# Expert stage of a mixture-of-experts block on one core: TensorE's order written by hand, and the second expert weight read in 8 KB runs

## The chip, the cores and the metric

One NeuronCore of one Trainium2 chip runs the whole block in one launch. The metric is the device time in microseconds (us). Lower is better. Three runs of the kernel before took 1494.55, 1496.63 and 1498.79 us; the median is 1496.63 us.

## The reference, cut to what matters

One layer of a diffusion backbone: modulated norm, a combined projection, two token mixers, an output projection, and then the part that the change touches, a mixture of 32 experts over 256 tokens of 1024 channels. Every token goes to its 4 best experts.

```python
def expert_block(args):                       # for every expert e, on its tokens
    xblk, e = args
    z = xblk @ w1[e] + b1[e]                  # w1: (32, 1024, 2048), float32
    gate = jnp.minimum(z[:, :D_EXPERT], SWIGLU_LIMIT)
    lin = jnp.clip(z[:, D_EXPERT:], -SWIGLU_LIMIT, SWIGLU_LIMIT)
    return (gate * jax.nn.sigmoid(SWIGLU_ALPHA * gate) * (lin + 1.0)) @ w2[e] + b2[e]   # w2: (32, 1024, 1024)
...
x = x + g2 * moe_ffn(modulate(x, norm2_g, sh2, sc2), ...)     # weighted sum of each token's experts
return rms_norm(x, final_g)
```

All weights are float32 and are read once: 8 MiB of w1 and 4 MiB of w2 for each expert, 384 MiB for the 32.

## The kernel before, in words

The first third (to about 500 us) computes the modulation, the projections, the mixers and the router, and isn't touched. The rest is the expert stage.

**Tiles.** Every expert has 64 slots (C = 64; a branch behind the loop serves experts with more tokens). `expert_rows` selects the tokens of two experts at a time and `gather` (L769) brings their activations into `xT2`, [channel, slot]. `expert_in` computes the first product: `zz` are two PSUM banks, gate and lin, opened by four small bias products (L791); then each of 8 tiles of w1 (128 rows of 2048 floats, 1 MiB, DMA at L795) is used by 4 products (L798), which stand in the trace as 8 MATMULs. The swiglu follows on VectorE and ScalarE (L803 to L807), the result is turned by four transposes (L810) and copied out by ScalarE (L812) as `hT2`. `expert_out` opens the bank `py` (L820), uses 4 tiles of w2 (1 MiB each, DMA at L824) with 8 MATMULs each (L828), multiplies by the gate g2 (`y`, L831), and scatters `y` back to the tokens with a one-hot matrix `pT` from `spread` (L780): four products (L840), each added into `acc` on VectorE (L843). The last expert's second product goes by columns, 256 at a time (`expert_out_by_columns`, L851 to L866), so that the final norm can begin early.

**The ring.** All weight tiles go through one ring of buffers of 8 KB a partition, in program order (`wtile`). SyncE (SP) issues their DMAs; each waits until TensorE has read the tile that had the buffer before. For the last two experts two buffers leave the ring, to hold rows that the end needs.

**The order.** Nothing in the expert stage is ordered by hand: the program is recorded expert by expert, and a scheduler with a simulated timeline places the instructions of each engine. In program order the second product of an expert stands right behind its swiglu.

**The layout of w2.** Row r of w2 sits on partition r % 128, so a tile of 256 rows gives each partition two runs of 4 KB:

```python
w = wtile([P, 2, D])
nc.sync.dma_start(w, w2e(k2).rearrange("(k p) n -> p k n", p=P))     # L824
```

A tile of w1 gives each partition one run of 8 KB; the last expert's column tiles give runs of 1 KB.

Of the kernel before, what the change touches and what calls it, by code (L numbers as in the profile page):

```python
# [16 lines left out]
P = 128  # L17
# [14 lines left out]
def kernel(  # L32
# [41 lines left out]
    def rstd_of(dst, ss, scale, tmp):  # L74
        """dst = (ss * scale + EPS) ** -0.5: a first guess from the exponent, then Newton steps."""
# [106 lines left out]
    def mod_sums(j, h):  # L182
        """Columns 512 h.. of part j for c, in two steps; still to be summed over partitions."""
# [65 lines left out]
    def modulation(q, w0=None):  # L249
        """md[:, j, a] = columns 256 q.. of part j (shift, scale) for c (a = 0) and c_ctx; a1 = (1 + scale) norm1_g"""  # L250
# [35 lines left out]
    class Granule:  # L286
        """256 columns of a (1024, n) matrix; pieces of k are split into two exact float32r parts."""
# [97 lines left out]
    def pair_dense(j, iv, q, og, sg):  # L385
        """The dense products of two heads, a granule a step."""
# [19 lines left out]
    def decays(hd, k, q):  # L406
        """The decayed queries and keys of a head; in [channel, token]."""
# [41 lines left out]
    def attend(hd, dec, iv, og):  # L449
        """Scores and states, output, and its norm and gate: three steps."""  # L450
# [299 lines left out]
    for tags, bufs in ((("sc0", "sc1", "py"), 1), (("gate",), 2), (("misc",), 1), (("lin",), 2)):  # L750
# [26 lines left out]
    def spread(sel, slot0):  # L777
        """[64 h + s, t] = 1 where token t has slot s + slot0 with the selected expert"""
# [6 lines left out]
    def expert_in(xT, selb, w1e):  # L785
        """swiglu(x w1 + b1) of the 64 tokens of xT; [channel, kt % 4, 64 (kt // 4) + slot]"""
# [6 lines left out]
        for kt in range(KT):  # L793
            w = wtile([P, 2 * D])
            nc.sync.dma_start(w, w1e(kt))  # L795
            for n in range(2):
                for h in range(2):
                    te.matmul(zz[n][h * C:(h + 1) * C], xT[:, kt], w[:, n * D + h * 512:n * D + (h + 1) * 512],  # L798
                              start=False, stop=kt == KT - 1, skip_group_check=True)
# [7 lines left out]
        ve.scalar_tensor_tensor(l, l, 1.0, g, op0=OP.add, op1=OP.mult)  # L807
        ph = bank2("misc", (P, 4, P))
        for k in range(4):
            te.transpose(ph[:, k], l[:, k * P:(k + 1) * P], ident)  # L810
# [4 lines left out]
    def expert_out(hT2, pT, selb, wcol, w2e, old=None):  # L815
        """acc = old + wcol * pT^T (g2 * (h w2 + b2))"""
# [14 lines left out]
        ve.tensor_mul(y, py, g2h)  # L831
        nonlocal acc
# [4 lines left out]
        for tt in range(2):  # L837
# [7 lines left out]
    def expert_out_by_columns(hT2, pT, selb, wcol, w2e):  # L845
        """The same, 256 columns at a time, with what the final norm needs of them; halves of py hold partial sums."""
        selb = selb.to_broadcast([96, C])
        for j in range(4):
            s = slice(j * 256, (j + 1) * 256)
            w = wtile([P, KT, 256])  # L850
            nc.sync.dma_start(w, w2e[:, s].rearrange("(k p) n -> p k n", p=P))  # L851
            py = bank2(("py", "misc")[j % 2], (P, 256))
            te.matmul(py[0:C], selb, b3[:, 2, s], start=True, stop=False, skip_group_check=True)
            for kt in range(KT):
                h = kt % 2
                te.matmul(py[h * C:(h + 1) * C], hT2[:, kt % 4, (kt // 4) * C:(kt // 4) * C + C], w[:, kt],
                          start=kt == 1, stop=kt >= KT - 2, skip_group_check=True)
            y = wk.tile([P, 256], F32, name="y")
            ve.tensor_mul(y, py, g2bc[:, s])
            for tt in range(2):  # L860
# [5 lines left out]
                (gp if j < 3 else ve).tensor_mul(accg[:, tt, s], acc[:, tt, s], fgbc[:, s])  # L866

    xT2 = p2 = None

    def expert_rows(e, n):  # L870
        """Selects and gathers for n experts from e."""
        m = e % 2
        for k in range(n):
            for tt in range(2):
                select(p2[:, tt, m + k], posm[:, tt, e + k:e + k + 1], tt)
        gather(p2[:, :, m:m + n].rearrange("p t a b -> p t (a b)"), xT2[:, :, m * C:(m + n) * C], n * C)

    late = []
    for e in range(E):
        if e == E - 2:  # L880
            slots[:] = [x for x in slots if x[1] not in ("d0", "d1")]
            bc = consts.tile([P, 2, D], F32, name="bc", tag="d0")
            fgbc, g2bc = bc[:, 0], bc[:, 1]
            gp.dma_start(fgbc, bcast(final_g, D))  # L884
            for h in range(2):
                pb = bank2("misc")
                te.matmul(pb, ident[:, h * C:h * C + 1].to_broadcast([P, P]), g2h, start=True, stop=True)
                sc.activation(g2bc[:, h * 512:(h + 1) * 512], pb, AF.Copy)
            accg = consts.tile([P, 2, D], F32, name="accg", tag="d1")
            ss8 = consts.tile([P, 2, 4], F32, name="ss8")  # L890
        if e % 2 == 0:
            p2 = wk.tile([P, 2, 2, C], F32, name="p2")
            xT2 = wk.tile([P, KT, 2 * C], F32, name="xT2")
            expert_rows(e, 1 if e == 0 else 2)
        elif e == 1:
            expert_rows(e, 1)
        if e == 0:
            ve.tensor_sub(lg, lg, view(top, 0, [[8, 2], [0, E]]))
            sc.activation(lg, lg, AF.Exp)
            ve.tensor_mul(wts, lg, mk)  # L900
            ve.reduce_sum(den, wts, axis=mybir.AxisListType.X)
            ve.reciprocal(den, den)
            for tt in range(2):
                ve.tensor_scalar(wts[:, tt], wts[:, tt], den[:, tt:tt + 1], None, op0=OP.mult)
        es = e % 2
        selb = sel96[:, e:e + 1]
# [3 lines left out]
        if e == E - 2:  # L910
            continue
# [96 lines left out]
```

## Time and profile before

| what | value |
|---|---|
| median of 3 runs | 1496.63 us (1494.55 to 1498.79) |
| span of the profiled execution | 1494.2 us |
| the profiled execution's own time | not listed apart; the three runs lie 0.4 to 4.6 us above its span, their median 2.4 us |
| PE busy over the span | 1371.3 us (92%) |
| DVE, ACT busy | 640.2 us (43%), 308.1 us (21%) |
| moved by DMA | 487.44 MB, mean 326 GB/s; 416 GB/s from 600 to 1395 us |

PE is TensorE's matmul, PEld its weight load, DVE VectorE, ACT ScalarE, SP SyncE. A MATMUL's end is modelled and neighbours overlap, so how long a kind of work takes is read from start to start in the timeline, not from the busy time. The DMA share is the busy share of the 16 DMA engines by the packets' own times; with two packets of an engine overlapping it goes over 1.

### The profile page before, as it was taken

How to read it: one execution, taken by the hardware profiler on the slowest of the kernel's cores; microseconds unless marked ns; L12 is line 12 of the kernel's file. 1: busy time of each engine (PE TensorE's matmuls, PEld its weight loads, DVE VectorE, ACT ScalarE, POOL GpSimd, SP SyncE). 2: the span in 40 equal slices, each digit the busy share in tenths (PEclk: the TensorE clock that was granted, in tenths of full speed). 3: DMA queues.
4: the chain of work that ended last, by engine and by line, in shares of the span. 5: the costliest groups of instructions: out<-in, count | busy, mean ns of one | idle time of the engine just before them, and what ended most of it. 6: DMA issues, size and time to landing. Idle time of an engine off the chain costs nothing. (4 is left out here: it accounts for less than half of the span.)

```text
span 1494.2 us, 19672 instructions
## 1 busy us (share of the span) xinstructions
PE 1371.3 (92%) x8218; PEld 760.8 (51%) x8218; DVE 640.2 (43%) x1108; ACT 308.1 (21%) x497; POOL 162.2 (11%) x109
## 2 busy tenths in 40 slices
PE   6979797979999989999999999998999989998996
PEld 4979797979999633343333233333333333333233
DVE  5598879697787421322323222222222222222124
ACT  3463535373444200000000000000000000001001
POOL 3054414240171000000000000000000000000001
PEclk8999999999999999999999999999999999999998
DMA  9536243435977799999999999999999999999970
GB/s 334 186 101 220 101 158 113 152 131 171 345 249 300 308 377 377 416 414 419 416 416 418 416 416 418 418 416 416 418 418 416 415 417 411 414 410 413 388 276 30
DMA packets 146560, 487.44 MB, mean 326 GB/s; under 512 B 9097, under 2 KB 71682, under 8 KB 113698
## 3 DMA queue, kind: packets, MB, share of 16 engines
q1 hardware_dynamic: 145618, 483.37, 83.1%
q0 software_dynamic: 848, 2.75, 0.6%
q8 instruction: 67, 1.10, 0.3%
q14 instruction: 27, 0.22, 0.0%
HBM read 485.04 MB, written 1.05 MB: 325 GB/s over the span
## 5 line engine op out<-in xcount | busy, mean ns | idle before, releaser
L798 PE MATMUL gate<-w,xT 128*64 128x512 f32 x1024 | 271.0, 598 | 4.0 <-DVE xT L775 4.0
L798 PE MATMUL lin<-w,xT 128*64 128x512 f32 x1024 | 272.1, 592 | 0.0
L828 PE MATMUL py<-w,hT 128*64 128x512 f32 x992 | 243.4, 634 | 16.1 <-ACT hT L812 16.1
L321 PE MATMUL acc<-hh,ghi 128*128 128x256 f32 x576 | 166.9, 290 | 12.1 <-ACT iv L394 12.1
L321 PE MATMUL acc<-hh,glo 128*128 128x256 f32 x576 | 165.5, 288 | 11.3 <-DVE glo L242 11.3
L321 PE MATMUL acc<-hl,ghi 128*128 128x256 f32 x576 | 165.1, 287 | 0.0
L242 DVE TENSOR_TENSOR glo<-w,ghi 128x1024 fp32r<-128x1024 f32 (+1 forms) x99 | 140.0, 1419 | 50.7 <-ACT ghi L241 50.3
L798 PEld LDWEIGHTS lin<-w,xT 128*64 128x64 f32 x1024 | 75.4, 137 | 148.4 <-issue 148.2
L828 PEld LDWEIGHTS py<-w,hT 128*64 128x64 f32 x992 | 71.2, 143 | 143.8 <-issue 115.9
L843 DVE SCALAR_TENSOR_TENSOR acc<-sc,wts,acc 128x512 f32<-128x512 f32 x124 | 89.0, 747 | 123.5 <-PE sc L840 123.4
L798 PEld LDWEIGHTS gate<-w,xT 128*64 128x64 f32 x1024 | 69.4, 136 | 127.1 <-issue 106.6
L241 ACT ACTIVATE ghi<-w 128x1024 fp32r<-128x1024 f32 (+1 forms) x102 | 102.3, 1007 | 144.6 <-PE acc L321 107.7
L321 PEld LDWEIGHTS acc<-hh,ghi 128*128 128x128 f32 x576 | 111.4, 194 | 13.3 <-ACT iv L394 12.5
L321 PEld LDWEIGHTS acc<-hh,glo 128*128 128x128 f32 x576 | 111.3, 193 | 12.9 <-DVE glo L242 12.6
L803 DVE TENSOR_SCALAR g<-gate 128x512 f32<-128x512 f32 x32 | 22.1, 692 | 212.1 <-PE gate L798 202.3
L321 PEld LDWEIGHTS acc<-hl,ghi 128*128 128x128 f32 x576 | 111.4, 193 | 0.7 <-issue 0.7
L804 ACT ACTIVATE s<-g 128x512 f32<-128x512 f32 x32 | 20.2, 630 | 423.6 <-DVE g L803 423.6
L884 POOL DMA_DIRECT2D bc<-in_final_g_dram x1 | 0.6, 557 | 934.7 <-DMA w<-in_w_dram 934.7
L831 DVE TENSOR_TENSOR y<-py,g2h 128x512 f32<-128x512 f32 x31 | 21.4, 692 | 165.0 <-PE py L828 165.0
L840 PE MATMUL sc<-y,pT 64*128 64x512 f32 x248 | 84.7, 641 | 8.0 <-DVE y L831 7.8
L321 PE MATMUL acc<-ghi,hh 128*128 128x256 f32 x256 | 73.3, 288 | 13.8 <-DVE og L383 6.3
L321 PE MATMUL acc<-glo,hh 128*128 128x256 f32 x256 | 73.1, 286 | 1.4 <-DVE glo L242 1.4
(320 smaller groups left out, 1656.1 us busy)
## 6 DMA issues: line engine op xcount, KB each, us to landing
w<-in_w_dram SPq DMA_DIRECT2D x384, 1024.0 KB, 13.7
w<-in_w_in_dram SPq DMA_DIRECT2D x33, 1024.0 KB, 5.7
w<-in_w_mod_dram SPq DMA_DIRECT2D x24, 1024.0 KB, 6.9
w<-in_w_branch_a_dram SPq DMA_DIRECT2D x4, 1024.0 KB, 16.3
w<-in_w_branch_b_dram SPq DMA_DIRECT2D x4, 1024.0 KB, 12.2
w<-in_w_out_dram SPq DMA_DIRECT2D x4, 1024.0 KB
w<-in_w_in_dram SPq DMA_DIRECT2D x12, 256.0 KB, 7.7
bt<-in_b_dram POOLq DMA_DIRECT2D x9, 128.0 KB, 5.0
```

What stands on the lines that cost most here:

```text
L241: sc.activation(hi, src, AF.Copy)
L242: eng.tensor_sub(lo, src, hi)
L321: te.matmul(o, l, r, start=opens and kt == 0 and n == 0, stop=kt == KT - 1 and n == 2, skip_group_check=True)
L798: te.matmul(zz[n][h * C:(h + 1) * C], xT[:, kt], w[:, n * D + h * 512:n * D + (h + 1) * 512], start=False, stop=kt == KT - 1, skip_group_c ...
L803: ve.tensor_scalar(g, zz[0], 7.0, None, op0=OP.min)
L804: sc.activation(s, g, AF.Sigmoid, scale=1.702)
L828: te.matmul(py[h * C:(h + 1) * C], hT2[:, kt % 4, (kt // 4) * C:(kt // 4) * C + C], w[:, k, h * 512:(h + 1) * 512], start=False, stop=kt = ...
L831: ve.tensor_mul(y, py, g2h)
L840: te.matmul(pcs[h], pT[h * C:(h + 1) * C, tt * P:(tt + 1) * P], y[h * C:(h + 1) * C], start=True, stop=True)
L843: ve.scalar_tensor_tensor(acc[:, tt, s], pcs[h], wcol[tt], old[:, tt, s], op0=OP.mult, op1=OP.add)
L884: gp.dma_start(fgbc, bcast(final_g, D))
```

## The change

`expert_in` and `expert_out` are cut into pieces (`w1_open`, `w1_step`, `swiglu`, `turned`, `w2_steps`, `scatter`, `last_columns`), and TensorE's instructions in the expert stage stand in the order in which the program writes them (`tc.manual_schedule`). The program now runs one expert behind with the second product: the first product of expert e, then its swiglu is recorded, then the second product of expert e - 1, then the transposes of e. The scatter of e - 2 stands behind the second and third tile of e's first product, and the gathers for the next two experts behind the fourth and sixth. The weights are allocated and read in that same order.

w2 is laid out anew: row 512 h + 4 p + k sits on partition p, so a tile gives each partition one run of 8 KB, and neighbouring partitions' runs lie 16 KB apart (the other half is read by the next tile). To match, the transposes read every fourth column of the swiglu's result. The last expert's column tiles keep runs of 1 KB, in two DMAs each. The PSUM pools change: gate and lin have one bank each in place of two, misc has three in place of one, and both halves of a gather go into misc. The two buffers leave the ring one expert later.

```diff
-    for tags, bufs in ((("sc0", "sc1", "py"), 1), (("gate",), 2), (("misc",), 1), (("lin",), 2)):
+    for tags, bufs in ((("sc0", "sc1", "py"), 1), (("gate",), 1), (("misc",), 3), (("lin",), 1)):
...
-    def gather(tok, xT, n):
-        for k4 in range(2):
-            pg = bank2(("misc", "sc0")[k4], (P, 4, n))
+    def gather(tok, xT, n, k4s=(0, 1)):
+        for k4 in k4s:
+            pg = bank2("misc", (P, 4, n))
...
+    def turned(l):
         ph = bank2("misc", (P, 4, P))
         for k in range(4):
-            te.transpose(ph[:, k], l[:, k * P:(k + 1) * P], ident)
+            te.transpose(ph[:, k], view(l, k, [[4, P]]), ident)
...
             w = wtile([P, 2, D])
-            nc.sync.dma_start(w, w2e(k2).rearrange("(k p) n -> p k n", p=P))
+            nc.sync.dma_start(w, w2e[:, k2 // 2, k2 % 2 * 2:k2 % 2 * 2 + 2])
...
-            nc.sync.dma_start(w, w2e[:, s].rearrange("(k p) n -> p k n", p=P))
+        for h in range(2):
+            nc.sync.dma_start(w[:, 4 * h:4 * h + 4], w2e[:, h, :, s])
...
+    w2e = lambda e: w2[0, e].rearrange("(h p k) n -> p h k n", h=2, k=4)
...
+    with tc.manual_schedule(engines={mybir.EngineType.PE}):
+        first_zz = w1_open(sel(0))
+        for f in rows_of(0, 1):
+            f()
+        for e in range(E):
...
+            zz = w1_open(sel(e)) if e else first_zz
+            for kt in range(KT):
+                w1_step(zz, xTs[e], kt, w1e(e, kt))
+                if kt in (1, 2) and ready:
+                    scatter(*ready[1:], x1 if ready[0] == 0 else None, (kt - 1,))
+                if kt == 3:
+                    steps = rows_of(1, 1) if e == 0 else rows_of(e + 1, 2) if e % 2 and e < E - 1 else []
+                if kt in (3, 5) and steps:
+                    steps[kt // 2 - 1]()
...
+            l = swiglu(zz)
+            if out_of:
+                pe, phT = out_of
+                pT = spread(identb[:, pe:pe + 1], 0)
+                y = w2_steps(phT, sel(pe), w2e(pe))
+                ready = pe, y, pT, wcols(pe)
+            out_of = e, turned(l)
+        e, hT2 = out_of
+        pT = spread(identb[:, e:e + 1], 0)
+        rest = last_columns(0, hT2, pT, sel(e), wcols(e), w2e(e))
+        scatter(*ready[1:])
+        for j in range(1, 4):
+            then = last_columns(j, hT2, pT, sel(e), wcols(e), w2e(e))
+            rest()
+            rest = then
+        rest()
```

TensorE at the turn from one expert to the next, in the middle of the stage, before. L791 opens the banks of the next first product, L810 are the transposes, L828 the second product, L780 the spread, L840 the scatter, L798 the next first product.

```order
L798 MATMUL lin<-w,xT_7833 64x512 x2
L791 LDWEIGHTS sel_69
...
L791 MATMUL lin<-b_4507,sel_69 64x512
L810 MATMUL misc<-ident,l 128x128 x4
L828 MATMUL py<-w,hT_7935 64x512 x8
L780 LDWEIGHTS identb
L780 MATMUL misc<-posT,identb 128x256
L828 MATMUL py<-w,hT_7935 64x512 x8
L840 MATMUL sc_7966<-y,pT 128x512
L840 MATMUL sc_7967<-y,pT 128x512
```

The same turn now (L800 is the first product, L836 the second, L818 the transposes, L852 the scatter).

```order
L800 MATMUL lin<-w,xT_7966 64x512 x2
L780 LDWEIGHTS identb
L780 MATMUL misc<-posT,identb 128x256
...
L836 MATMUL py<-w,hT_8067 64x512 x16
L818 MATMUL misc<-ident,l 128x128 x4
L791 LDWEIGHTS sel_69
...
L800 MATMUL gate<-w,xT_7966 64x512 x2
L800 MATMUL lin<-w,xT_7966 64x512 x2
L852 MATMUL sc_8201<-y,pT 128x512
L852 MATMUL sc_8202<-y,pT 128x512
```

Before, the transposes and the second product stood straight behind the swiglu that they need, and the scatter behind the product that makes `y`. Now the 16 products of the expert before stand between the swiglu and its transposes, and the transposes, the bank openings and two tiles stand between `y` and its scatter.

SP's queue of weight DMAs from its start in the expert stage, before and now, as one piece of the difference (L824 and L832 read w2, L795 and L797 w1).

```order
-L795 DMA w<-in_w_dram 128x2048 x9
-L920 TENSOR_LOAD maxc
-L920 ISA x2
-L824 DMA w<-in_w_dram 128x2x1024 x4
-L795 DMA w<-in_w_dram 128x2048 x8
-L824 DMA w<-in_w_dram 128x2x1024 x4
-L795 DMA w<-in_w_dram 128x2048 x9
-L824 DMA w<-in_w_dram 128x2x1024 x3
-L795 DMA w<-in_w_dram 128x2048 x3
```

```order
L797 DMA w<-in_w_dram 128x2048 x8
L832 DMA w<-in_w_dram 128x2048 x4
L797 DMA w<-in_w_dram 128x2048 x8
L832 DMA w<-in_w_dram 128x2048 x4
```

A w2 tile is now one row of 2048 floats a partition, where it was two of 1024, and after the first tiles the queue holds 8 tiles of w1 and 4 of w2 in turn, in the order in which TensorE reads them.

## Rows read from the trace of the kernel before

**Rows 1.** Section 1 of the page: busy time, share of the span and instructions of each engine.

```profile
span 1494.2 us, 19672 instructions
PE 1371.3 (92%) x8218; PEld 760.8 (51%) x8218; DVE 640.2 (43%) x1108; ACT 308.1 (21%) x497; POOL 162.2 (11%) x109
```

**Rows 2.** Busy time by stretch: the stretch, its length, busy time and count of PE, PEld, DVE, ACT, POOL, then the granted clock, the DMA share and GB/s.

```profile
510.00:600.00 90.00, 85.44 (x392) 32.08 (x390) 18.13 (x38) 7.59 (x14) 0.00 (x0) 0.96 0.98 377
600.00:800.00 200.00, 196.25 (x922) 73.79 (x919) 55.75 (x99) 15.31 (x28) 0.00 (x0) 0.99 1.02 417
800.00:1395.00 595.00, 547.13 (x2514) 193.56 (x2513) 151.54 (x270) 41.62 (x78) 0.56 (x1) 0.98 1.02 416
1395.00:1437.00 42.00, 39.57 (x177) 14.45 (x175) 9.14 (x15) 3.34 (x6) 0.00 (x0) 0.96 0.92 359
1437.00:1449.00 12.00, 11.46 (x53) 3.78 (x53) 3.16 (x6) 2.14 (x4) 0.00 (x0) 1.00 1.03 339
1449.00:1483.00 34.00, 32.79 (x177) 15.49 (x176) 11.23 (x21) 3.66 (x12) 3.27 (x5) 1.00 0.03 9
```

**Rows 3.** The same view for the instructions on the weight tiles w alone (8 MATMULs read one tile of 1 MiB), same columns.

```profile
600.00:800.00 200.00, 152.95 (x670) 48.92 (x666) 0.00 (x0) 0.00 (x0) 0.00 (x0) 0.99 1.02 417
800.00:1395.00 595.00, 426.40 (x1834) 125.72 (x1835) 0.00 (x0) 0.00 (x0) 0.00 (x0) 0.98 1.02 416
```

**Rows 4.** Waits of SP's queue from 600 to 1395 us: who waited for whom, us in total, times, longest.

```profile
SPq L824 <- PE lin L798: 175.2, 87, 4.0
SPq L795 <- PE py L828: 171.8, 71, 6.5
```

**Rows 5.** Busy time by stretch again: two stretches in which w1 alone lands (8 KB runs), two in which w2 alone lands (4 KB runs), and one of the last expert's columns (1 KB runs).

```profile
675.00:701.00 26.00, 26.00 (x123) 10.46 (x125) 8.09 (x17) 2.39 (x5) 0.00 (x0) 1.00 1.01 420
897.00:912.00 15.00, 15.00 (x72) 4.62 (x68) 3.51 (x5) 0.00 (x0) 0.00 (x0) 1.00 1.02 423
...
655.00:661.00 6.00, 6.00 (x30) 1.98 (x28) 2.67 (x4) 0.63 (x1) 0.00 (x0) 1.00 1.03 410
727.00:734.00 7.00, 6.77 (x30) 2.13 (x28) 5.36 (x8) 1.23 (x2) 0.00 (x0) 1.00 1.03 410
...
1441.00:1448.00 7.00, 6.60 (x34) 2.34 (x32) 2.67 (x4) 1.23 (x2) 0.00 (x0) 1.00 1.07 349
```

**Rows 6.** Timeline at a turn between experts: start us, us, engine, line, operation, out<-in, count, and in brackets the idle time before and what ended it. The last row is the swiglu's first step two experts later.

```profile
1036.79 0.69 DVE L803 TENSOR_SCALAR g<-gate 128x512 f32<-128x512 f32 x1 [8.20 <-PE gate L798]
...
1038.39 0.41 PE L791 MATMUL lin<-b,sel 96*64 96x512 bf16 x2 [0.45 <-DVE l L805]
...
1039.72 0.66 PE L810 MATMUL misc<-ident,l 128*128 128x128 f32 x4 [0.92 <-DVE l L807]
...
1041.06 1.94 PE L828 MATMUL py<-w,hT 128*64 128x512 f32 x8 [0.69 <-ACT hT L812]
...
1098.38 0.69 DVE L803 TENSOR_SCALAR g<-gate 128x512 f32<-128x512 f32 x1 [9.91 <-PE gate L798]
```

**Rows 7.** Timeline of PE, same columns, for the time from start to start of each kind of work, and from the list of groups the addition that follows a scatter (busy us, mean ns of one, idle before).

```profile
1022.90 1.13 PE L840 MATMUL sc<-y,pT 64*128 64x512 f32 x4
1023.96 0.41 PE L820 MATMUL py<-b,sel 96*64 96x512 bf16 x2
1024.20 1.03 PE L798 MATMUL gate<-w,xT 128*64 128x512 f32 x4
...
1026.02 1.13 PE L840 MATMUL sc<-y,pT 64*128 64x512 f32 x4
...
1052.28 0.28 PE L780 MATMUL misc<-posT,identb 32*128 32x256 bf16 x1
1052.48 1.13 PE L840 MATMUL sc<-y,pT 64*128 64x512 f32 x4
...
1396.71 1.03 PE L798 MATMUL gate<-w,xT 128*64 128x512 f32 x4
1397.57 1.03 PE L798 MATMUL lin<-w,xT 128*64 128x512 f32 x4
1398.42 1.03 PE L798 MATMUL gate<-w,xT 128*64 128x512 f32 x4
...
1421.72 2.05 PE L769 MATMUL misc<-p,acc 128*128 128x128 f32 x16
1423.70 1.13 PE L840 MATMUL sc<-y,pT 64*128 64x512 f32 x4
...
1446.34 0.66 PE L810 MATMUL misc<-ident,l 128*128 128x128 f32 x4 [0.40 <-DVE l L807]
1446.93 1.08 PE L798 MATMUL gate<-w,xT 128*64 128x512 f32 x4
...
L843 DVE SCALAR_TENSOR_TENSOR acc<-sc,wts,acc 128x512 f32<-128x512 f32 x124 | 89.0, 747 | 123.5 <-PE sc L840 123.4
```

**Rows 8.** A stretch of 15 us with one turn between experts, columns as in rows 2.

```profile
1125.00:1140.00 15.00, 12.94 (x55) 3.92 (x53) 3.16 (x5) 1.23 (x2) 0.00 (x0) 0.89 1.03 414
```

**Rows 9.** Timeline: the start of the first expert on PE, the last column product, and the output's DMAs.

```profile
508.83 1.08 PE L798 MATMUL gate<-w,xT 128*64 128x512 f32 x4
...
1479.34 2.01 PE L856 MATMUL misc<-w,hT 128*64 128x256 f32 x16
...
1488.41 1.83 SPq L969 DMA_DIRECT2D out_dram<-accg  x4
```

More of the change, by code (lines that the diff above doesn't have):

```diff
@@ L783, in spread, with w1_open @@
         return pT
-    def expert_in(xT, selb, w1e):
+    def w1_open(selb):
         zz = [bank2("gate"), bank2("lin")]
@@ L792, in expert_in, with w1_step, swiglu @@
                           skip_group_check=True)
[L793 to L799, printed above, removed]
+        return zz
+    def w1_step(zz, xT, kt, src):
+        w = wtile([P, 2 * D])
+        nc.sync.dma_start(w, src)
+        for n in range(2):
+            for h in range(2):
+                te.matmul(zz[n][h * C:(h + 1) * C], xT[:, kt], w[:, n * D + h * 512:n * D + (h + 1) * 512],
+                          start=False, stop=kt == KT - 1, skip_group_check=True)
+    def swiglu(zz):
         g = wk.tile([P, 512], F32, name="g", bufs=1)
@@ L813, in expert_in, with w2_steps @@
         return hT2
-    def expert_out(hT2, pT, selb, wcol, w2e, old=None):
+    def w2_steps(hT2, selb, w2e):
         selb = selb.to_broadcast([96, C])
@@ L831, in expert_out, with scatter @@
         ve.tensor_mul(y, py, g2h)
+        return y
+    def scatter(y, pT, wcol, old=None, tts=(0, 1)):
         nonlocal acc
@@ L836, in expert_out @@
             old = acc
-        for tt in range(2):
+        for tt in tts:
             pcs = [bank2(f"sc{h}") for h in range(2)]
@@ L866, in expert_out_by_columns, with rows_of @@
                 (gp if j < 3 else ve).tensor_mul(accg[:, tt, s], acc[:, tt, s], fgbc[:, s])
[L868 to L890, printed above, removed]
+        return rest
+    tok, xTs = {}, {}
+    def rows_of(e, n):
         if e % 2 == 0:
@@ L893 @@
             xT2 = wk.tile([P, KT, 2 * C], F32, name="xT2")
[L894 to L902, printed above, removed]
-            for tt in range(2):
-                ve.tensor_scalar(wts[:, tt], wts[:, tt], den[:, tt:tt + 1], None, op0=OP.mult)
@@ L905 @@
-        es = e % 2
-        selb = sel96[:, e:e + 1]
-        pT = spread(identb[:, e:e + 1], 0)
-        hT2 = expert_in(xT2[:, :, es * C:(es + 1) * C], selb, lambda kt: w1[0, e, kt * P:(kt + 1) * P])
-        late.append((hT2, pT, selb, [wts[:, tt, e:e + 1] for tt in range(2)]))
-        if e == E - 2:
-            continue
-        for i, args in enumerate(late):
-            ee = e - len(late) + 1 + i
-            if ee == E - 1:
-                expert_out_by_columns(*args, w2[0, ee])
-            else:
-                expert_out(*args, lambda k2: w2[0, ee, k2 * 256:(k2 + 1) * 256], None if ee else x1)
@@ L918 @@
-        late = []
+            for k in range(2):
+                tok[e + k], xTs[e + k] = p2[:, :, k], xT2[:, :, k * C:(k + 1) * C]
+        else:
+            p2, xT2 = tok[e], xTs[e]
+        for k in range(n):
+            for tt in range(2):
+                select(tok[e + k][:, tt], posm[:, tt, e + k:e + k + 1], tt)
+        if n == 2:
+            t, x = p2.rearrange("p t a b -> p t (a b)"), xT2
+        else:
+            t, x = tok[e], xTs[e]
+        return [lambda k4=k4: gather(t, x, n * C, (k4,)) for k4 in range(2)]
@@ L946 @@
                 pT = spread(one[:E], C * blk)
-                hT2 = expert_in(xT, one[:96], lambda kt: w1[0, bass.ds(er, 1), kt * P:(kt + 1) * P]
-                                .rearrange("a p n -> (a p) n"))
-                expert_out(hT2, pT, one[:96], [pw[:, 1, tt:tt + 1] for tt in range(2)],
-                           lambda k2: w2[0, bass.ds(er, 1), k2 * 256:(k2 + 1) * 256].rearrange("a p n -> (a p) n"))
+                zz = w1_open(one[:96])
+                for kt in range(KT):
+                    w1_step(zz, xT, kt, w1[0, bass.ds(er, 1), kt * P:(kt + 1) * P].rearrange("a p n -> (a p) n"))
+                y = w2_steps(turned(swiglu(zz)), one[:96], w2[0, bass.ds(er, 1)]
+                             .rearrange("a (h p k) n -> p (a h) k n", h=2, k=4))
+                scatter(y, pT, [pw[:, 1, tt:tt + 1] for tt in range(2)])
         for tt in range(2):
```

50 lines of the change are left out of this document (38 added, 12 removed).

## The prediction

> **What bounds the kernel now.** I read the page's busy shares first [rows 1]: PE is busy 92% of the span, which says nothing yet about who waits for whom, because ends of MATMULs are modelled. The view by stretch says more [rows 2]. From 600 to 1395 us the DMA engines look full (share 1.02, 416 to 417 GB/s), so the expert stage seems to be bound by its transfers. Two other views speak against that as the whole answer. SP's queue waits for PE to give buffers back, 175.2 + 171.8 us in its two largest rows [rows 4]. And PE's own pace, counted in weight tiles, is the slower one: from 800 to 1395 us it reads 1834 / 8 = 229.3 tiles in 595 us, 2.595 us a tile, where the transfers bring one in 1.0486 MB / 416 GB/s = 2.521 us [rows 3, 2]. From 600 to 800 us PE was quicker (670 / 8 = 83.8 tiles, 2.388 us each) [rows 3]. So PE falls behind through a ring of some 20 buffers, and the transfers look full only because the ring still has room. It shows at the end: the rate falls to 359 GB/s from 1395 us on, the last byte has landed by 1449 us, and PE still works until 1483 us [rows 2]. Transfers and PE are within 3% of each other, and PE ends last.
>
> PE's pace holds waits that are no work. Two experts take 1098.38 - 1036.79 = 61.6 us, 30.8 each [rows 6]. At each turn PE waits for the swiglu: 0.45 us for the bank, 0.92 us for the swiglu's result, 0.69 us for ScalarE's copy, 2.06 us in all [rows 6].
>
> **What the change does to PE.** From start to start at the full clock [rows 7]: a tile of 8 MATMULs 1398.42 - 1396.71 = 1.71 us, 12 of them 20.5; a scatter half 1.06 us, and the tile ahead of it takes 1026.02 - 1024.20 = 1.82, so two halves cost 2 x 1.17 = 2.3; spread 0.20; the bank openings 0.24 a pair, three pairs 0.7; transposes 0.59; a gather half 1423.70 - 1421.72 = 1.98 plus 0.1 of switching, two halves for two experts, 2.1 an expert. The sum is 26.4 us of work an expert. The new order leaves nothing else: behind the swiglu stand 16 products (4 x 1.71 = 6.9 us) where its chain on VectorE and ScalarE needs 2.06 us plus the openings; ahead of a scatter stand transposes, openings and two tiles, 5 us, where `y` needs about 0.8; the two halves are apart by a tile of 1.71 us, where the two additions between them take 2 x 0.747 [rows 7]. With one bank each for gate and lin the openings wait for the swiglu's reads, which are over 6 us earlier. The transposes now read every fourth column; the trace has no such read. Below nothing there is no reason; at worst I take them at four times their 0.59, 1.8 us an expert. PE would then need 28.2.
>
> **What it does to the transfers.** 8 KB runs land at 420 and 423 GB/s, 4 KB runs at 410 [rows 5]. I take 421 for w2 in its new layout: a tile takes 2.491 us in place of 2.558, 0.067 x 124 = 8.3 us over 31 experts. No row shows 8 KB runs that lie 16 KB apart. The bounds are w1's best 423 (4 us less in the sum below) and the columns' 349 [rows 5], which also skip memory between runs; I stay with 421 because the run's length is w1's. The number of tiles and the ring are as before. An expert's 12 tiles need 29.9 us, PE 26.4 to 28.2, so **the transfers now set the pace**, PE works off its backlog of some 20 tiles at about 3 us an expert, and from the middle of the stage on it waits for each tile.
>
> The Trainium skill, page "DMA: Bandwidth & Descriptors", section "Why small descriptors are slow (HBM only)", gives a packet about 3 cycles beside its beats of 32 bytes; by that, 4 KB runs would lose only 1.2% against 8 KB, an estimate from the page, and the sum would come out near 1451 us in place of the time below. The rows show 2.7%, and the measured number is the one used.
>
> **The sum.** From 510 us to the last byte the kernel before moves 90 x 377 + 200 x 417 + 595 x 416 + 42 x 359 + 12 x 339 + 34 x 9 = 384.3 MB [rows 2]. The change moves the same: 4.2 MB of columns at 349 GB/s, 12.0 us, and 380.1 MB at 421, 902.9 us. From 510 to 600 us the kernel before lost 90 x (417 - 377) / 417 = 8.6 us to a PE that gave buffers back late [rows 2]; the first swiglu still has nothing to stand in front of it, so I keep 2 us of that. The last byte lands at 510 + 914.9 + 2 = 1427 us, 22 us earlier than before.
>
> Behind it, the last column product needs 1 us for its second half. Ahead of it stand two scatter halves back to back, the second of which waits for two additions of 0.747 us [rows 7], and the products and scatters of the columns; since these columns come only 3.0 us apart, I put PE 3 us behind there. From the end of that product, 1479.34 + 2.01 = 1481.35, to the span's end, the kernel before needs 1494.2 - 1481.35 = 12.9 us [rows 9, 1], most of it the norm and the output; that is unchanged. So the tail behind the last byte is 17 us where it was 1494.2 - 1449 = 45. The span is 1427 + 17 = 1444, **50 us less**: 22 from the transfers' end (8 from the layout, 14 from a queue that no longer waits for buffers) and 28 from the backlog that is gone. The median of the runs is 2.4 us above the profiled span of 1494.2; with that the forecast is 1446 us.
>
> PE has room for this: 508.8 [rows 9] + 32 x 26.4 = 1354 us, 73 us ahead of the last byte. SP, VectorE, ScalarE and POOL lie under it: their work per expert is what it was. The row broadcasts for the final norm (two products and two copies) move into the last expert, where PE waits for tiles anyway.
>
> **Rivals.** *w2 gains nothing from its layout*, or less: at 410 GB/s the sum is 8.3 us longer, 1454. For it: only w1 shows the better rate, in memory read without a gap. Chance 0.20.
>
> *PE stays near the bound.* A PE that waits for each tile idles, and the clock may fall. One stretch with 2.06 us of idle time had a granted clock of 0.89 over 15 us, 1.65 us lost as part of it ran at 1.2 in place of 2.4 GHz [rows 8]. Two such falls an expert cost 3.3 us; with the 26.4 that makes 29.7, and PE just follows; with slow transposes too it is 31.5, more than the transfers need. Against it: a PE that falls behind is busy again and stops idling. I give 1458 to 1488 a chance of 0.09; the upper end is also what comes out if the transfers were the true bound already and only the layout counts (1496.6 - 8.3).
>
> *Nothing changes* (1492 to 1501): the hand-written order brings a wait of its own, about 3 us at each turn, for instance a VectorE whose order doesn't fit. The order shown speaks against it. 0.04.
>
> *Slower, by the transfers of w2.* If it is the skipped memory and not the 1 KB run that makes the column tiles slow, the new w2 tiles land at 349 GB/s too: 3.005 us in place of 2.491, 124 x 0.514 = 63.7 us, 1510 us. This decides once a w2 tile takes 0.445 us more than I take, below 357 GB/s: then 1446 + 55 = 1501 is passed. Against it: the column tiles' packets are an eighth as long, which alone can explain the rate, and in the old layout a partition's two runs lie 512 KB apart and still land at 410. 0.06. The Trainium skill, page "DMA: Bandwidth & Descriptors", section "Latency and other measured facts", tells of copies that lose rate when partitions read at a pitch of a large power of two; its pitches begin far above 16 KB, and no run here shows one.
>
> **How the numbers follow.** The forecast has 0.61: 1438 to 1453 by itself, from 423 GB/s (4 us less), no loss at the start (2 less) and no lag in the columns (3 less) on the one side, and a few us of a low clock at the tail on the other. 0.3%, 4.5 us, is about what a measurement of this kernel can tell from no change. Faster has 0.61 + 0.20 + 0.09 = 0.90, the same 0.04, slower 0.06. The range that holds 8 in 10 takes in the forecast, w2 without gain, and the near half of a PE that stays close: 1437 to 1468 us.
>
> **What would show it.** In the profile after: waits of PE at the turns gone, no idle time on `hT`, the swiglu or `y`; PE's idle time ended by DMA of w in the second half of the stage; SP's waits for PE small there, replaced by waits for its own transfers; stretches of w2 at 421 GB/s like those of w1; the last byte near 1427 us and 17 us behind it. It is wrong if w2's stretches stay at 410 or fall below, if PE still has tiles to read 30 us after the last byte, or if the granted clock falls through the second half and PE's tiles take longer than 2.49 us.

## The result, and the profile after

Side by side, four runs each, the kernel before took 1497.71 us (1494.55 to 1499.64) and the changed kernel **1453.51 us** (1450.91 to 1456.02): ratio 0.9719, 95% interval [0.9687, 0.9752], 44 us less. In a later set of runs, beside the kernels of the last sections, it took 1452.49 us (1448.24 to 1460.13), ratio 0.9714 [0.9674, 0.9755]. The ratio is always to the kernel before, run beside it. The profiled execution took 1452.21 us, with a span of 1450.4; of the four runs, the two that took longer (1454.8 and 1456.02 us) had a mean granted clock of 0.977, the other two 0.983 and 0.984.

Section 1 of the page after, to hold against [rows 1]:

```profile
span 1450.4 us, 19638 instructions
PE 1345.7 (93%) x8218; PEld 743.0 (51%) x8218; DVE 640.0 (44%) x1108; ACT 307.9 (21%) x497; POOL 161.1 (11%) x109
```

The share of PE has not moved (92% before, 93% now), and yet another resource is the bound. The busy shares don't tell that. The view by stretch does; columns as in [rows 2], the last four rows are the last expert's columns:

```profile
510.00:600.00 90.00, 87.88 (x450) 35.60 (x448) 22.55 (x48) 10.24 (x19) 0.00 (x0) 1.00 0.99 404
600.00:800.00 200.00, 200.00 (x968) 71.60 (x966) 56.76 (x100) 15.30 (x28) 0.00 (x0) 1.00 1.01 421
800.00:1395.00 595.00, 557.71 (x2612) 191.18 (x2608) 153.42 (x272) 42.82 (x80) 0.56 (x1) 1.00 1.01 421
...
1415.00:1420.00 5.00, 3.95 (x18) 0.97 (x16) 0.28 (x1) 0.00 (x0) 0.00 (x0) 1.00 0.80 303
1420.00:1425.00 5.00, 4.13 (x24) 1.84 (x24) 1.17 (x2) 0.60 (x1) 0.00 (x0) 1.00 1.01 334
1425.00:1430.00 5.00, 4.16 (x23) 1.61 (x21) 2.65 (x5) 0.00 (x0) 0.00 (x0) 1.00 0.92 305
1430.00:1435.00 5.00, 5.00 (x39) 3.77 (x36) 2.11 (x5) 1.02 (x4) 1.41 (x2) 1.00 0.10 32
```

And for the weight tiles alone, as in [rows 3]:

```profile
600.00:800.00 200.00, 162.80 (x726) 49.39 (x722) 0.00 (x0) 0.00 (x0) 0.00 (x0) 1.00 1.01 421
800.00:1395.00 595.00, 449.65 (x1912) 125.07 (x1912) 0.00 (x0) 0.00 (x0) 0.00 (x0) 1.00 1.01 421
```

From 600 to 800 us PE is busy without a gap and reads 726 / 8 = 90.75 tiles. That is 2.204 us each or 26.4 us an expert, the figure of the prediction, but the stretch does not begin and end with an expert. From one opening of `py` to the next but one, PE needs 733.88 - 680.01 = 53.87 us, which is 26.9 us an expert, 0.5 more than summed:

```profile
680.01 0.41 PE L828 MATMUL py<-b,sel 96*64 96x512 bf16 x2
...
733.88 0.41 PE L828 MATMUL py<-b,sel 96*64 96x512 bf16 x2
```

From 800 us on it reads 1912 / 8 = 239 tiles in 595 us, 2.490 us each: that is the transfers' 1.0486 MB / 421 GB/s = 2.491. So PE worked off its backlog and then ran at the transfers' pace. The waits say the same. The waits of PE's MATMULs from 840 to 1395 us, all of them (who waited for whom, us in total, times, longest):

```profile
PE py L836 <- DMA w<-in_w_dram: 19.1, 40, 1.0
PE gate L800 <- DMA w<-in_w_dram: 16.3, 28, 1.6
```

SP's from 600 to 1395 us, the four largest, against [rows 4]:

```profile
SPq L797 <- DMA w<-in_w_dram: 435.3, 209, 3.6
SPq L832 <- DMA w<-in_w_dram: 213.0, 102, 3.6
SPq L797 <- PE lin L800: 10.5, 23, 2.4
SPq L832 <- PE lin L800: 8.0, 7, 2.5
```

SP hardly waits for PE to give a buffer back (some 29 us in all, against 347 us in the two rows of before); it waits for its own transfers. A turn between experts in the timeline, against [rows 6]; in brackets the idle time ahead of an instruction and what ended it:

```profile
1053.19 0.69 DVE L807 TENSOR_SCALAR g<-gate 128x512 f32<-128x512 f32 x1 [1.22 <-PE gate L800]
...
1054.38 5.32 PE L836 MATMUL py<-w,hT 128*64 128x512 f32 x24
...
1055.76 0.69 DVE L811 SCALAR_TENSOR_TENSOR l<-l,g 128x512 f32<-128x512 f32 x1
...
1059.92 1.94 PE L836 MATMUL py<-w,hT 128*64 128x512 f32 x8 [0.22 <-DMA w<-in_w_dram]
...
1061.79 0.39 PE L818 MATMUL misc<-ident,l 128*128 128x128 f32 x1
```

The swiglu runs from 1053.19 to 1056.45 beside the 32 MATMULs of the second product of the expert before. Its result is there 5.3 us ahead of the transposes. The three waits of [rows 6], 2.06 us a turn, are gone; one of 0.22 us for a tile stands there now.

### The profile page after: what moved, and what is told of

It reads as the page before. It is cut to its first block, busy times and chain, and to the rows that moved or that the text cites. A ratio compares the mean times of both kernels' runs of the same rounds, so it can differ in the third digit from the quotient of the medians.

```text
span 1450.4 us, 19638 instructions
## 1 busy us (share of the span) xinstructions
PE 1345.7 (93%) x8218; PEld 743.0 (51%) x8218; DVE 640.0 (44%) x1108; ACT 307.9 (21%) x497; POOL 161.1 (11%) x109
## 5 line engine op out<-in xcount | busy, mean ns | idle before, releaser
L800 PE MATMUL gate<-w,xT 128*64 128x512 f32 x1024 | 270.4, 606 | 18.6 <-DMA w<-in_w_dram 17.2
L800 PE MATMUL lin<-w,xT 128*64 128x512 f32 x1024 | 263.5, 592 | 0.0
L836 PE MATMUL py<-w,hT 128*64 128x512 f32 x992 | 228.1, 597 | 20.8 <-DMA w<-in_w_dram 20.8
L321 PE MATMUL acc<-hh,glo 128*128 128x256 f32 x576 | 165.5, 288 | 11.3 <-DVE glo L242 11.3
L836 PEld LDWEIGHTS py<-w,hT 128*64 128x64 f32 x992 | 66.3, 136 | 162.8 <-issue 98.6
L800 PEld LDWEIGHTS lin<-w,xT 128*64 128x64 f32 x1024 | 74.3, 137 | 145.5 <-issue 145.5
L800 PEld LDWEIGHTS gate<-w,xT 128*64 128x64 f32 x1024 | 61.0, 136 | 163.6 <-issue 96.6
L773 ACT ACTIVATE xT<-misc,sh,a 128x128 f32<-128x128 f32 (+1 forms) x68 | 30.7, 451 | 272.4 <-DVE xT L775 272.4
L775 DVE TENSOR_SCALAR xT<-misc,a,sh 128x128 f32<-128x128 f32 (+1 forms) x68 | 27.2, 401 | 131.0 <-PE misc L769 120.5
```

What stands on the lines that cost most here:

```text
L321: te.matmul(o, l, r, start=opens and kt == 0 and n == 0, stop=kt == KT - 1 and n == 2, skip_group_check=True)
L773: sc.activation(xT[:, kt], pg[:, k], AF.Identity, bias=sh2[:, kt:kt + 1], scale=a2[:, kt:kt + 1])
L775: ve.tensor_scalar(xT[:, kt], pg[:, k], a2[:, kt:kt + 1], sh2[:, kt:kt + 1], op0=OP.mult, op1=OP.add)
```

## Experiments

### What each half of the change gives alone

Hand-written order and lag, but w2 as before, two 4 KB runs a partition, and one DMA for each of the last expert's columns:

```diff
-            te.transpose(ph[:, k], view(l, k, [[4, P]]), ident)
+            te.transpose(ph[:, k], l[:, k * P:(k + 1) * P], ident)
...
-            nc.sync.dma_start(w, w2e[:, k2 // 2, k2 % 2 * 2:k2 % 2 * 2 + 2])
+            nc.sync.dma_start(w, w2e[:, 2 * k2:2 * k2 + 2])
...
-        for h in range(2):
-            nc.sync.dma_start(w[:, 4 * h:4 * h + 4], w2e[:, h, :, s])
+        nc.sync.dma_start(w, w2e[:, :, s])
...
-    w2e = lambda e: w2[0, e].rearrange("(h p k) n -> p h k n", h=2, k=4)
+    w2e = lambda e: w2[0, e].rearrange("(k p) n -> p k n", p=P)
```

> TensorE's hand-written order and the lag of one expert as in the change, but w2 in the old layout (two 4 KB runs a partition, whole column tiles, transposes of neighbouring columns). My theory: the transfers set the pace in the new order, so w2 at 410 GB/s in place of 421 costs all of its 124 x 0.067 = 8.3 us: 1453.5 + 8.3 = 1462 us, ratio 0.976. The rate from 600 to 1395 us goes back to 417 GB/s, and TensorE keeps waiting for tiles in the second half. Rival, the layout is worth nothing by itself: 1453 us. Second rival, the order is worth little without the layout: over 1480 us.

Measured: 1459.34 us, ratio 0.9762 [0.9732, 0.9792]. By stretch:

```profile
600.00:800.00 200.00, 200.00 (x971) 70.52 (x969) 57.24 (x101) 14.99 (x28) 0.00 (x0) 1.00 1.02 417
800.00:1395.00 595.00, 549.24 (x2576) 185.72 (x2576) 151.34 (x269) 42.25 (x79) 0.00 (x0) 1.00 1.02 417
```

And the new layout in the kernel before, with the scheduler's order (and two DMAs a column, as in the change):

```diff
-            te.transpose(ph[:, k], l[:, k * P:(k + 1) * P], ident)
+            te.transpose(ph[:, k], view(l, k, [[4, P]]), ident)
...
-            nc.sync.dma_start(w, w2e(k2).rearrange("(k p) n -> p k n", p=P))
+            nc.sync.dma_start(w, w2e[:, k2 // 2, k2 % 2 * 2:k2 % 2 * 2 + 2])
...
-            nc.sync.dma_start(w, w2e[:, s].rearrange("(k p) n -> p k n", p=P))
+            for h in range(2):
+                nc.sync.dma_start(w[:, 4 * h:4 * h + 4], w2e[:, h, :, s])
```

> The scheduler's order as before, w2 in the new layout alone (8 KB runs, transposes of every fourth column). My theory: TensorE set the pace before, at 30.8 us an expert, so faster transfers only make it wait for buffers earlier: no change, 1494 to 1499 us, with the rate from 800 to 1395 us unchanged at 415 to 417 GB/s because SP waits for buffers. Rival, the transfers set the pace before: 8.3 us less, 1489 us (ratio 0.994).

Measured: 1496.08 us, ratio 1.0005 [0.9983, 1.0028].

```profile
600.00:800.00 200.00, 196.10 (x919) 74.40 (x917) 55.39 (x99) 15.59 (x29) 0.00 (x0) 0.99 1.01 421
800.00:1395.00 595.00, 547.25 (x2490) 195.57 (x2488) 148.51 (x266) 40.68 (x76) 0.56 (x1) 0.97 1.00 410
```

The same 8 KB runs are worth nothing alone. Behind the new order they are worth 0.9719 / 0.9762 = 0.9956, some 6.5 us; by the two intervals that is 0.991 to 1.000, and the traces bear it out with 421 in place of 417 GB/s and a span of 1450.4 in place of 1457.5 us. The two rows of this run show why they gain nothing alone: in the old order the transfers run at 421 GB/s for as long as the ring has room, then wait for PE and fall to 410 (I had expected 415 to 417 there). A faster transfer only fills the ring sooner.

### The skipped memory in w2's new layout

A tile is laid out as one closed block of 256 rows of w2 (row 256 b + 2 p + k on partition p), so that neighbouring runs of 8 KB touch; each of the last expert's columns then takes four DMAs:

```diff
-            te.transpose(ph[:, k], view(l, k, [[4, P]]), ident)
+            te.transpose(ph[:, k], view(l, k // 2 * 256 + k % 2, [[2, P]]), ident)
...
-            nc.sync.dma_start(w, w2e[:, k2 // 2, k2 % 2 * 2:k2 % 2 * 2 + 2])
+            nc.sync.dma_start(w, w2e[:, k2])
```

> As the change, but a w2 tile is one closed block of 256 rows, two neighbouring rows a partition (row 256 b + 2 p + k): runs of 8 KB that lie one behind the other, with no memory skipped; transposes of every second column; column tiles in four DMAs of 256 KB. My theory: the length of the run sets the rate, so nothing changes: 421 GB/s, 1450 to 1457 us. Rival, the skipped memory costs something: a rate of 423 or more in w2's stretches and 3 us or more off.

Measured: 1452.98 us, ratio 0.9714 [0.9678, 0.9751], 421 GB/s from 600 to 1395 us as in the change. The gaps cost nothing that shows; the rival that made the kernel slower falls.

### The lag without the hand-written order, and the order without the lag

First the second product straight behind its own swiglu, with TensorE still ordered by hand:

```diff
-            l = swiglu(zz)
-            if out_of:
-                pe, phT = out_of
...
-            out_of = e, turned(l)
+            pT = spread(identb[:, e:e + 1], 0)
+            hT2 = turned(swiglu(zz))
+            if e < E - 1:
+                ready = e, w2_steps(hT2, sel(e), w2e(e)), pT, wcols(e)
```

> The change's hand-written order and layout, but without the lag of one expert: the second product of an expert stands straight behind its own swiglu and transposes (its scatter stays behind the second and third tile of the next expert). My theory: TensorE waits again at each turn, for the swiglu (about 2.3 us) and for ScalarE's copy (0.7), and now and then a low clock follows, so an expert takes 26.8 + 3.0 + 0.6 = 30.4 us, more than the 29.9 of the transfers: TensorE paces the stage and keeps its backlog, about 1485 to 1497 us. Rival, a fixed order that agrees with the DMA queue's is what counts, lag or not: 1453 to 1462 us.

Measured: 1508.53 us, ratio 1.008 [1.005, 1.0111], 0.8% slower than the kernel before and slower than both theories had it. PE at a turn, and a stretch of 15 us around it:

```profile
1019.86 0.75 PE L818 MATMUL misc<-ident,l 128*128 128x128 f32 x4 [2.30 <-DVE l L811]
...
1021.30 8.78 PE L836 MATMUL py<-w,hT 128*64 128x512 f32 x32 [0.35 <-ACT hT L820]
1029.91 0.39 PE L791 MATMUL gate<-b,sel 96*64 96x512 bf16 x2
```

```profile
1020.00:1035.00 15.00, 14.65 (x64) 4.88 (x65) 0.69 (x1) 0.60 (x1) 0.00 (x0) 0.89 1.01 418
```

PE waits 2.30 + 0.35 = 2.65 us, where the scheduler's order had 2.06 in three pieces. Then the granted clock is 0.89, and four tiles take 1029.91 - 1021.30 = 8.61 us in place of 4 x 1.71 = 6.84: a part of them ran at 1.2 in place of 2.4 GHz. So this turn costs 2.65 + 1.77 = 4.4 us. Not every turn loses its clock: from 840 to 1395 us PE waits 47.8 us at 18 turns, and the granted clock is 0.97 in the mean, which is 0.03 x 555 / 18 = 0.9 us a turn. I had expected 30.4 us an expert, with 3.0 for the waits and 0.6 for the clock; the openings of `py` come 30.7 us apart, so that part was about right.

The rest of the miss lies in the first experts. In the kernel before the scheduler lags by itself there: it places tiles of a further first product in front of the transposes, and from 600 to 780 us PE waits 1.8 us in all. Here the waits stand at every turn from the start, 15.9 us in the same stretch, and from 600 to 800 us PE is busy for 184 us in place of 196 [rows 2]:

```profile
600.00:800.00 200.00, 184.05 (x868) 68.14 (x866) 50.16 (x91) 13.76 (x26) 0.00 (x0) 0.97 1.00 411
```

This run keeps the new layout, the PSUM pools and the places of gathers and scatters, so none of these brings the gain without the lag.

Then the other way: the program text with the lag is kept, and the scheduler places TensorE's instructions.

```diff
-    with tc.manual_schedule(engines={mybir.EngineType.PE}):
+    if True:
```

> The change without the hand-written order on TensorE: the program text with the second product one expert behind, and w2 in 8 KB runs, are kept, and the scheduler places TensorE's instructions again. In its order one tile (1.71 us) of the second product stands between the swiglu and the transposes, and a scatter often straight behind its product. Theory (the lag is what counts, not who writes the order): PE needs 26.4 + about 1.2 us of waits = 27.6 an expert, still under the transfers' 29.9; 1451 to 1460, ratio .969 to .975. Rival (the hand-written order itself is worth the gain): back to 1485 to 1500, ratio .992 or more.

Measured: 1449.31 us, ratio 0.9727 [0.9702, 0.9752]. To read it within a few us it ran again with the unedited change beside it:

> The changed kernel itself, unedited, beside the next two on one chip, so that differences of a few us can be read. Expected: ratio to before .972 (.969 to .975), as in its first runs.

> The change without the hand-written order (the scheduler places TensorE's instructions, the second product one expert behind), once more, now beside the change itself. Theory (the lag carries the gain, the transfers set the pace either way): within 3 us of the changed kernel. Rival (the hand order costs or gives something beyond that): a difference of more than 4 us, either way.

Measured: the change 1452.49 us, 0.9714 [0.9674, 0.9755]; the lag alone 1450.22 us, 0.9702 [0.966, 0.9743]. No difference shows. In the scheduler's order PE does have small waits, of 840 to 1395 us these:

```profile
PE gate L800 <- DMA w<-in_w_dram: 16.6, 33, 0.7
PE lin L791 <- DVE l L809: 8.6, 19, 0.5
PE sc L852 <- DVE y L839: 7.9, 10, 0.8
```

The two that wait for VectorE take 16.5 us of a room that is far larger, and cost nothing. **The lag carries the gain; who writes the order down does not matter here.** (No run has the lag in the scheduler's order with the old layout.)

### How much room PE has

Products whose result nobody reads, one and three an expert:

```diff
+                if kt in (6,):                 # pe_plus3: (4, 6, 7)
+                    te.matmul(bank2("misc"), ident[:, 0:1].to_broadcast([P, P]), g2h, start=True, stop=True)
```

> The change, with one extra product per expert on TensorE whose result nobody reads (fp32 128x512, about 1.05 us, behind the seventh tile of the first product): some 34 us more of PE work in all. Theory (the transfers set the pace, PE has about 1.7 us to spare per expert): the time stays within 2 us of the change's 1453.5 (ratio to before .971 +- .002), PE's waits for DMA of w shrink by about as much as the work grows. Rival (PE still ends last, or a wait of PE is on the path): 34 us longer, about 1487 (ratio .993).

> The change, with three such unread products per expert (about 3.2 us an expert, some 101 us in all), behind the fifth, seventh and eighth tile. Theory: PE's room of about 54 us up to the end of the last but one expert is used up, and what is left shows: 101 - 54 = 47 us more, about 1500 (1490 to 1512, ratio 1.002); SP waits for PE again, PE no longer waits for tiles. Rival 'PE sets the pace already': +101, about 1555. Rival 'PE has room of over 3 us an expert': no change, 1454.

Measured: one product 1455.19 us, ratio 0.9763 [0.9738, 0.9788]; three 1499.03 us, ratio 1.0066 [1.0034, 1.0099]. In that set of runs the kernel before took 1492.14 us, in the others 1493.5 to 1498.1, so the first ratio is above the range that was expected while the time lies in it. By the ratios the loss is 0.9763 / 0.9719, some 6.5 us. The trace shows 5 of them: the rate from 510 to 600 us is 380 GB/s in place of 404, 90 x 24 / 421 = 5 us, where PE has no room yet and its granted clock is 0.98 in place of 1.00. PE's waits for tiles from 840 to 1395 us shrink from 35.4 to 12.9 us, as expected. Against the 34 us that a PE-bound kernel would show, 2 to 6.5 is small.

With three products the room is used up. They cost more than the 3.2 us an expert that I took: two experts need 1067.54 - 1006.74 = 60.80 us, where the change needs 53.87 while PE has no wait. That is 3.47 us an expert, 111 us in all.

```profile
1006.74 0.41 PE L828 MATMUL py<-b,sel 96*64 96x512 bf16 x2
...
1067.54 0.41 PE L828 MATMUL py<-b,sel 96*64 96x512 bf16 x2
```

The 111 us of work cost 1499.0 - 1453.5 = 45.5 us, so the room is some 65 us, where 54 was worked out. That the time came out as expected is in part luck: the work and the room were both some 10 us larger than taken. SP's waits in that run, 600 to 1395 us:

```profile
SPq L797 <- PE lin L800: 258.6, 104, 3.4
SPq L832 <- PE lin L800: 230.1, 105, 3.4
SPq L797 <- PE py L836: 177.9, 104, 2.9
```

SP waits for PE again and PE for nothing: PE has become the bound once more, seen from the other side.

### The start and the end

Two places in the trace of the change still have PE waiting with nothing in front. At the first turn there is no second product to stand there (PE, change):

```profile
528.04 0.75 PE L818 MATMUL misc<-ident,l 128*128 128x128 f32 x4 [2.12 <-DVE l L811]
```

And PE at the end, from the last tile of the last but one expert:

```profile
1420.88 1.94 PE L836 MATMUL py<-w,hT 128*64 128x512 f32 x8 [0.62 <-DMA w<-in_w_dram]
1422.74 0.75 PE L818 MATMUL misc<-ident,l 128*128 128x128 f32 x4
...
1424.18 1.95 PE L868 MATMUL py<-w,hT 128*64 128x256 f32 x16 [0.25 <-ACT hT L820]
1426.06 1.13 PE L852 MATMUL sc<-y,pT 64*128 64x512 f32 x4
1428.02 1.78 PE L852 MATMUL sc<-y,pT 64*128 64x512 f32 x4 [0.84 <-DVE acc L855]
...
1429.74 2.01 PE L868 MATMUL misc<-w,hT 128*64 128x256 f32 x16
...
1432.76 2.01 PE L868 MATMUL py<-w,hT 128*64 128x256 f32 x16
...
1435.77 2.01 PE L868 MATMUL misc<-w,hT 128*64 128x256 f32 x16
```

The end first. The transposes go between the second and third tile ahead, the columns come in four tiles with 2 KB runs, and the scatter halves stand apart:

```diff
+            if k2 == 2 and between:
+                between()                      # the last expert's transposes
...
-        w = wtile([P, KT, 256])
-        for h in range(2):
-            nc.sync.dma_start(w[:, 4 * h:4 * h + 4], w2e[:, h, :, s])
+        for hh in range(2):
+            w = wtile([P, 4, 512])
+            nc.sync.dma_start(w, w2e[:, hh, :, c * 512:(c + 1) * 512])
...
+                if not c and i == hh:
+                    between[hh]()              # one half of the scatter
```

> The change with another end: the last expert's transposes stand between the second and third tile of the second product ahead of them, its columns are read in four 1 MB tiles with runs of 2 KB (in place of eight DMAs with runs of 1 KB), and the two scatter halves stand apart among the column products. Worked out from the trace of the change: PE's chain from the last tile at 1420.9 to the end of the column products is 1.7 + 0.4 + 3.9 + 2.1 + 1.95 + 2.1 + 1.95 = 14.1 us, to 1435.0, where it was 1437.7: 2.7 us less, 1451 us, ratio .970. Rival (the transfers of the columns bind the tail, and 2 KB runs land at 400 GB/s in place of 320): up to 5 us less, 1448. Rival (the tail hangs on VectorE and the output alone): no change.

Measured: 1450.18 us, ratio 0.9731 [0.9709, 0.9752], in the same set, with the kernel before at 1492.14. The time is as worked out, the trace less so: from the last tile's start to the end of the column products it needs 1421.01 to 1436.53, 15.5 us, where the change needs 1437.78 - 1420.88 = 16.9. So 1.4 of 2.7 us came; 0.74 is a wait for VectorE ahead of the fourth column. Taken by itself this run shows no gain that its interval could tell. The next one mends that wait, and fills the start:

```diff
-                if kt in (3, 5) and steps:
+                if kt in (3, 5) and steps and e:
...
             l = swiglu(zz)
+            if e == 0:
+                for f in steps:
+                    f()
...
-                if not c and i == hh:
+                if not c and i == 0:
```

> The change with two edits where PE still has nothing in front of a wait. Start: the gathers for the second expert (2 x 1 us) move behind the first expert's swiglu, the one turn with no second product in front of the transposes; theory: up to 2 us of PE's wait filled while the ring is still full, so the rate from 510 to 600 us rises from 404 towards 410 GB/s. End: as in the run tail2 (transposes inside the second product ahead, columns in 2 KB runs, scatter halves apart), with the second scatter half one product earlier, so that VectorE's 0.74 us wait there goes; 2.7 us there. In all 3 to 5 us under the changed kernel on the same chip, ratio to before .968 to .970. Rival (the end hangs on VectorE and the output, and the start on the first third of the kernel): within 2 us of the changed kernel.

Measured: 1445.22 us (1444.6 to 1448.05), ratio 0.9661 [0.9626, 0.9696], 7.3 us under the unedited change in the same set: 0.5% faster than the change; its slowest run lies below the fastest of the change there (1448.24). The start edit alone:

> The change with the start edit of the run tail3 alone (the second expert's gathers behind the first expert's swiglu), to split that run's 7.3 us. Theory (the start gave 3.4 us by its rates, 510 to 600 us at 418 GB/s in place of 403, the new end about 2, the rest an earlier first product): 1448 to 1450 us, ratio .968 to .970, 418 GB/s from 510 to 600 us, and the last expert's end as in the changed kernel. Rival (the end gave it all): 1452 to 1453.

Measured: 1448.49 us, ratio 0.9689 [0.966, 0.9717]. The stretch at the start and PE at the first turn:

```profile
510.00:600.00 90.00, 90.00 (x463) 36.37 (x461) 25.37 (x53) 9.60 (x20) 0.00 (x0) 1.00 1.01 418
```

```profile
520.99 3.79 PE L769 MATMUL misc<-p,acc 128*128 128x64 f32 x32
524.61 0.68 PE L818 MATMUL misc<-ident,l 128*128 128x128 f32 x4
```

No wait is left there: the gathers stand in it, and the rate goes from 404 to 418 GB/s: 90 x 14 / 421 = 3.0 us. That leaves 3 to 4 us for the new end, of which the trace of tail3 shows 16.9 - 14.6 = 2.3 (1415.35 to 1429.92). Single steps of this size are at the edge of what the runs tell; the two together are beyond it.

## Why the prediction was right, and where its sizes were off

**What bounds.** Right. PE had set the pace before, by waits and not by work. The prediction's parts did not add up to that pace, though: 26.4 of work and 2.06 of waits are 28.5 us an expert, where it read 30.8. By the trace of before PE waits 45 us at the 18 turns from 840 to 1395 us, 2.5 each, and the granted clock of 0.98 there is another 0.6; with 26.9 of work that makes 30.0, and some 0.8 us stays open. With the waits gone it needs 26.9 us an expert, where 26.4 were summed, and the transfers set the pace at 29.9, so the half microsecond costs nothing. The room of some 65 us, order and lag alone at 0.9762 and the layout alone at 1.0005 all follow from that, and were put down beforehand as 54 us, 0.976 and no change. The time by itself would not tell: 1453.5 us is half a microsecond above the forecast's own 1438 to 1453, and is what the rival "w2 gains nothing" gave, 1454. The rate of w2 decides between the two.

**Where the gain comes from.** Right in kind: the transfers' end came 18 to 19 us earlier, and the tail behind it is 20 us in place of 45. The layout's term was 8.3 us; the runs with and without it differ by about 6.5, their spans by 7.1. From 600 us on the rates, 421 and 417 GB/s, are as taken; the columns of the run without it (order_only) landed faster than those of the change, at 320 to 357 GB/s.

**The rate of w2.** Right: 421 GB/s from 600 to 1395 us, and the same with closed blocks. The mix of two thirds at 421 and one third in 4 KB runs lands at 417, which puts 4 KB runs at 1 / (3 / 417 - 2 / 421) = 409 GB/s, 2.8% under 8 KB. The estimate of 1.2% from the Trainium skill, page "DMA: Bandwidth & Descriptors", section "Why small descriptors are slow (HBM only)", is too small here; the measurement decides.

**Clock.** The rival said that a PE that waits for each tile loses its clock. It does not in this form: from 840 to 1395 us PE waits 68 times, for every third tile or so, half a microsecond each on the mean, and the granted clock stays 1.00. The kernel without the lag shows that the mechanism exists: one wait of 2.30 us, and 0.89. It doesn't follow every such wait: at the first turn, which is the same in the change and in tail2, the row from 525 to 540 us has a granted clock of 1.00 and 347 GB/s in the one and 0.89 and 298 GB/s in the other.

**What was off.** The span came out at 1450.4 in place of 1444, three terms of the sum:
- The start, taken as 2 us, cost 90 x (421 - 404) / 421 = 3.6. The first turn keeps its full wait, and SP waits there for PE to give buffers back; from 525 to 540 us the rate is 347 GB/s. The start_fill run removes most of it.
- The columns, taken at 349 GB/s [rows 5], landed at 303 to 334: a loss of 15 x (421 - 314) / 421 = 3.8 us where 2.0 was in the sum. The last byte came at some 1430.5 in place of 1427 (the row from 1430 us on has 5 x 32 = 160 KB left). The change cut each column's DMA in two, but the runs speak against that as the reason. With the same two DMAs a column pe_plus3 has 350 GB/s; with four, contiguous has 320; with one, order_only has 320 to 357. The columns in pe_plus3 and in contiguous:

```profile
1432.00:1443.00 11.00, 11.00 (x56) 4.03 (x57) 2.24 (x4) 0.60 (x1) 0.56 (x1) 1.00 1.10 350
...
1416.00:1431.00 15.00, 12.03 (x59) 4.54 (x61) 3.95 (x7) 0.60 (x1) 0.00 (x0) 1.00 0.93 320
```

  What goes with the low rates in these runs is one long issue on SP. SP's issues of the columns in the change, in the kernel before and in order_only (ns, shortest, median, longest):

```profile
L863 SPq DMA_DIRECT2D w<-in_w_dram x8: 615/1386/8897, 1403.4 to 1423.8; - x8
```

```profile
L851 SPq DMA_DIRECT2D w<-in_w_dram x4: 367/368/1582, 1434.7 to 1442.5; - x4
```

```profile
L862 SPq DMA_DIRECT2D w<-in_w_dram x4: 2708/3134/11281, 1410.2 to 1428.0; - x4
```

  In the change the long one lasts from 1408.8 to 1417.7 us, and from 1416 to 1419 us the rate is 269 GB/s. In pe_plus3, where PE sets the pace, the longest issue is 2.0 us.

- The lag of PE in the columns, taken as 3 + 1 us behind the last byte, was 7. From the first column to the second PE needs 1429.74 - 1424.18 = 5.56 us, with both scatter halves and the 0.84 us wait between them; then 3.0 a column, a product of 1.95 and a scatter of 1.06. It never catches up. The 12.9 us behind it held: 1450.4 - 1437.8 = 12.6.

1444 + 1.6 + 1.8 + 3 = 1450.4. What stays open is why an issue lasts that long, and whether it is the whole reason of the columns' lower rate: in layout_only, with two DMAs a column and no issue above 0.9 us, the columns landed at 313 GB/s, while SP waited 6.6 us for PE. With four tiles of 1 MB in 2 KB runs (tail2) the rate from 1415 to 1425 us was 365 and 367 GB/s, but there number and run length changed together.

**What I credited wrongly.** Title and prediction give the gain to the new order as written by hand. The runs give it to the lag in the program; the hand-written order without the lag is slower than the kernel before (1.008 [1.005, 1.0111]).

## What to carry to other kernels

When two engines are within a few per cent of each other, count pace in the unit that both share (here us a weight tile), not busy time, and price each edit against the slower one: the 8 KB runs were worth nothing until PE had stopped setting the pace. Put the next independent work in front of a dependent chain by lagging the program by one stage; a scheduler can then do the placing. Waits that are free in the middle of a pipeline still cost in full at its first and last turn, and that is where to look next.

## What the runs showed of the hardware

- Idle time in 68 pieces of about 0.5 us, one for every third tile or so, left the granted clock at 1.00 for 555 us (the change). In no_lag one piece of 2.3 us at a turn went with 0.89 over the 15 us around it, and 1.77 us lost; at the first turn a piece of 2.1 us went with 1.00 in the change and with 0.89 in tail2.
- Runs of 8 KB that lie 16 KB apart land at 421 GB/s, as closed blocks do.
- How long SP is held as it issues a DMA in runs of 1 KB is not set by the DMA alone: 1 MB took 0.4 to 1.6 us in the kernel before and 2.7 to 11.3 us in order_only, 512 KB took 0.6 to 2.0 us in pe_plus3 and 0.6 to 8.9 us in the change. 1 MB in runs of 8 KB took 0.33 to 0.39 us (w1 in the change).
